# Latents, rotary keys and p: transposes by VectorE in 32x32 blocks instead of TensorE, in one inference step on one core

## The chip, the cores and the metric

The kernel runs on one core of a Trainium2 chip. The metric is the device time of one execution in microseconds (us); the median of several runs is given. The core has five engines that run side by side: TensorE (PE; its weight loads are shown apart as PEld), VectorE (DVE), ScalarE (ACT), GpSimd (POOL) and SyncE (SP), which here issues nearly all DMA transfers. Each engine works through its own queue in order, and waits at an instruction until what it needs is there.

## The reference, cut to what matters

One layer of a decoder for a prompt of 1024 tokens and 8 sampled sequences of 4 tokens each. The rows that the change touches:

```python
z = rmsnorm(x, ln_w) @ w_in
rq, rk, rv, rg, cq, ckv, kr, mg, ga, gb = jnp.split(z, ...)
q = (rmsnorm(cq, q_norm_w) @ w_uq).reshape(b, s, MLA_HEADS, MLA_QK)
ckv = rmsnorm(ckv, kv_norm_w)
kr = rope(kr, pos)                       # one rotary key of 64 for all heads
...
kv = (ckv @ w_ukv).reshape(b, s, MLA_HEADS, MLA_NOPE + MLA_V)
sc = einsum('bqhd,bkhd->bhqk', qn, k_nope) + einsum('bqhr,bkr->bhqk', qr, kr)   # masked softmax, then @ v
...
x = x + merged @ w_out
return x + jax.nn.sigmoid(x @ w_ple_gate) * (ple @ w_ple_proj)                 # ple is p, 256 wide
```

cq (384 wide), ckv (256) and kr (64) together are the 704 columns called latents here. The rest (retention with its state, paged attention of the samples, gates, the output projections) is computed too, and is not touched.

## The kernel before, in words

Arithmetic is done on pairs of fp32r tiles (a high part and the rest, `h` and `l`); a product is three matmuls (`mac`, lines 266 to 268). Matmuls need the contracted dimension on the 128 partitions. So what is computed with tokens on partitions has to be transposed before it can be multiplied further.

The stages, in order of time:

1. Latents, 0 to about 145 us. The prompt is worked through in 8 tiles of 128 tokens, and a ninth of 32 for the samples, in the order 0, 1, 8, 2 to 7. For a tile, `load_x` asks for x, `turn_tile` transposes it on TensorE (8 transposes, copied out of PSUM to `turn`, stored to `xTD`) and takes its norm, `scale_tile` makes `y` and the pair `xn`, and `latent_tile` multiplies by the latents' weights (48 matmuls into two PSUM tiles `ac`) and makes `la`: norms, rotation of the key (`rope_nat`, tiles `kro`), stores to the outputs. Then come, with a delay of one tile (the `yield` in `latent_tile` and `due` in `latents`), five transposes of `la` on TensorE, copies to `lt`, and a store to `latD`. The rotary key goes untransposed to `krD`. `turn_p` loads 128 rows of p to `pl`, has TensorE transpose them (two transposes), copies and stores them to `pTD`. The product `fill` (gates ga, gb, silu gates; tiles `mm`, results `gev`) is woven in from the seventh tile on.
2. First queries of the samples (weights `early`), paged attention with the rest of `fill` beside it, to about 750 us; retention, to about 1360 us.
3. Latent attention of the prompt, 8 heads, from about 1360 us. Latents are loaded transposed from `latD` (tiles `lat`, split to `lh` and `ll`). `rope_keys` transposes the key `krN` on TensorE and makes the pair `krA`, `krB`, each twice on 64 partitions. `prep` of a head is woven into the attention of the head before. For a block of 128 queries `probabilities` computes scores in `ac`, their maximum `mx` and minus that as `nm` (VectorE), the exponential `pr` (ScalarE) and the scaling by `rl` (GpSimd); `attend` transposes and multiplies by the values.
4. Output projections, to the end, where `embedding` loads p transposed from `pTD`.

The tile framework orders each engine's queue ahead of time, by a simulated schedule; so a change in one place moves instructions in its neighbourhood. Tiles of one tag form a ring of `bufs` buffers: a new one waits until the oldest is read. `wst` holds the rings of weights (`wr`, 2 buffers; `wh`, `wl`) and `gev` (2).

The pattern that the change uses is in the kernel already, for the retention's keys: VectorE's transpose turns each 32x32 block in place, and four stores, one for each group of 32 partitions, put the blocks where they belong in DRAM:

```python
dve.transpose(st, dst[m][:, j * TH:j * TH + n].rearrange("p (b r) -> p b r", r=32))
for a in range(0, P, 32):
    sp.dma_start(kD[h % 2][bs, :, m * P + a:m * P + a + 32].rearrange("b i f -> i b f"), st[a:a + 32])
```

Of the kernel before, what the change touches and what calls it, by code (L numbers as in the profile page):

```python
# [9 lines left out]
F32 = mybir.dt.float32  # L10
# [9 lines left out]
P = 128  # L20
# [141 lines left out]
def decode_step(ctx: ExitStack, tc: tile.TileContext, A: dict, O: dict):  # L162
# [57 lines left out]
    latD = dram.tile([P, 5, SEQ], F32, tag="latD", name="latD")  # L220
    xTD = dram.tile([P, 8, NT], F32, tag="xTD", name="xTD")
    pTD = dram.tile([P, 2, NT], F32, tag="pTD", name="pTD")
    krD = dram.tile([P, 8, ROPE], F32, tag="krD", name="krD")
# [104 lines left out]

    def turn_p(t):
        n = rows(t)  # L330
        pl = p1.tile([P, PLE], F32, tag="pl", name="pl", bufs=2)
        sp.dma_start(pl[:n], A["p_prompt"][0, 0, t * P:(t + 1) * P, :] if t < 8 else A["p_sample"].rearrange("l b t c -> (l b t) c"))
        turn_input(t, pl, pTD, PLE // P)
# [47 lines left out]
    def latent_tile(t):  # L381
# [15 lines left out]
        if t < 8:  # L397
            sp.dma_start(O["ckv_prompt"][0, 0, t * P:(t + 1) * P, :], kv)
            sp.dma_start(O["krope_prompt"][0, 0, t * P:(t + 1) * P, :], la[:, QL + KL:])
            sp.dma_start(krD[:, t, :], la[:, QL + KL:])  # L400
            yield
            pt, pt2 = tr(), tr()
            for i in range(3):
                pe.transpose(pt[:, i * P:(i + 1) * P], la[:, i * P:(i + 1) * P], ident)
            for i in range(2):
                pe.transpose(pt2[:, i * P:(i + 1) * P], la[:, (3 + i) * P:(4 + i) * P], ident)
            lt = p1.tile([P, 5, P], F32, tag="lt", name="lt", bufs=2)
            act.copy(lt[:, 0:3, :], pt[:, :3 * P].rearrange("p (a b) -> p a b", a=3))
            dve.tensor_copy(lt[:, 3:5, :], pt2[:, :2 * P].rearrange("p (a b) -> p a b", a=2))
            sp.dma_start(latD[:, :, t * P:(t + 1) * P], lt)  # L410
        else:
            sp.dma_start(O["ckv_sample"].rearrange("l b t c -> (l b t) c"), kv)
            sp.dma_start(O["krope_sample"].rearrange("l b t c -> (l b t) c"), la[:n, QL + KL:])
# [47 lines left out]
    def latents():  # L461
        due = iter(())
        for n, t in enumerate(order):
            tile_ = latent_tile(t)
            if 0 < n < 7:
                turn_tile(order[n + 2])
            next(tile_, None)
            run(due)
            due = tile_
# [4 lines left out]
            if n + 4 < 9:  # L474
                load_x(order[n + 4])
            turn_p(t)
# [6 lines left out]
        run(due)  # L483
# [598 lines left out]
    for h in range(HR):  # L1082
# [5 lines left out]
        if h + 1 < HR:  # L1088
            rest = (head_in(h + 1, nxt), 50.3)
        else:  # L1090
            rest = (gate_tiles(C_MG, mgD, range(5, 8), AF.Silu), 31.8)
            raws = [(qkB if i < 4 else qkA)("lat", (P, SEQ), F32) for i in range(5)]
            for i, raw in enumerate(raws):
                sp.dma_start(raw, latD[:, i, :])
            krN = qkA("krN", (P, 8, ROPE), F32)
            sp.dma_start(krN, krD)
# [43 lines left out]
    def rope_keys():  # L1140
        for u in range(2):
            pt = tr()
            us = slice(u * 512, (u + 1) * 512)
            for i in range(4):
                pe.transpose(pt[:ROPE, i * P:(i + 1) * P], krN[:, 4 * u + i, :], ident)
            act.copy(krA[0:ROPE, us], pt[:ROPE])
            act.copy(krA[ROPE:P, us], pt[:ROPE])
            lo_of(krB[0:ROPE, us], pt[:ROPE], krA[0:ROPE, us])
            act.copy(krB[ROPE:P, us], b32(krB[0:ROPE, us]))
            yield 0.43  # L1150
# [213 lines left out]
    waiting = []  # L1364
    for h in range(HM):
# [15 lines left out]
        for n, m in enumerate((3, 2, 0, 1)):  # L1381
# [9 lines left out]
            waiting.append(unit)  # L1391
            if h + 1 == HM:
# [92 lines left out]
    def embedding(j):  # L1485
        pT = [xs_("pT", (P, 2, TH)) for _ in range(2)]
        for k in range(2):
            hi, lo = (pT[k][:, i, :] for i in range(2))
            raw = xs_("pTr", (P, TH), F32)
            sp.dma_start(raw, pTD[:, k, j * TH:(j + 1) * TH])  # L1490
# [139 lines left out]
```

## Time and profile before

| | |
|---|---|
| median of 3 runs | 2164.25 us (2162.3 to 2164.99) |
| profiled execution | 2169.16 us |
| its span, first to last instruction | 2167.2 us |
| mean granted TensorE clock | 0.997 |
| TensorE busy | 2123.5 us, 15258 matmuls and transposes |
| VectorE busy | 1255.8 us |
| ScalarE busy | 730.7 us |
| DMA | 307.59 MB, mean 142 GB/s |

A row of the profile names line, engine and operation, output<-inputs by the program's names, shapes and count; then times. A busy TensorE is not one at its peak, as matmuls are pipelined: a matmul's printed length is longer than the distance to the next one's start, which is called its pitch below. Idle time in square brackets stands with the instruction that ended it and the operation that released it.

### The profile page before, as it was taken

What the parts mean: (1) busy time and instruction counts of PE and PEld (TensorE: products, weight loads), DVE (VectorE), ACT (ScalarE), POOL (GpSimd) and SP (SyncE); (2) the same over time, 40 slices, a digit from 0 to 9 for tenths busy, and PEclk for the clock granted to TensorE, in tenths of its full rate; (3) what the DMA queues carried; (4) which work ended last, traced back from release to release, by engine and by line L of the source; (5) the groups of instructions that cost most, each with busy time, mean ns of one, the idle gap of its engine ahead of it and who ended that gap; (6) DMA issues with size and microseconds to landing.
All of it is one profiled execution on the core that took longest, in us unless ns stands there. A gap on an engine that the chain in (4) does not pass through costs nothing.

```text
span 2167.2 us, 38594 instructions
## 1 busy us (share of the span) xinstructions
PE 2123.5 (98%) x15258; PEld 1847.5 (85%) x15258; DVE 1255.8 (58%) x2823; ACT 730.7 (34%) x1535; POOL 328.0 (15%) x519
## 2 busy tenths in 40 slices
PE   8999999999999999999999999899999999999998
PEld 7988777777777897888888887788888999999998
DVE  5524564565646346666676774778777353444465
ACT  6412222333334222222222221454556342222243
POOL 2210111111110022222122220122221000000022
PEclk9999999999999999999999999999999999999999
DMA  8557656566655432453634627110112453234243
GB/s 232 146 162 256 227 205 225 179 249 214 215 201 195 128 85 66 153 161 98 224 72 123 199 72 260 44 37 12 38 53 71 142 189 99 86 93 125 79 142 118
DMA packets 302693, 307.59 MB, mean 142 GB/s; under 512 B 61296, under 2 KB 260080, under 8 KB 298416
## 3 DMA queue, kind: packets, MB, share of 16 engines
q1 hardware_dynamic: 293296, 221.23, 33.6%
q0 software_dynamic: 9216, 83.89, 10.3%
q8 instruction: 120, 1.97, 0.4%
q14 instruction: 61, 0.50, 0.1%
HBM read 236.70 MB, written 68.36 MB: 141 GB/s over the span
## 4 chain that ended last, share of the span: by engine, by line
PE 63%; DVE 3%; issue 3%; ACT 1%; POOL 1%; DMA 1%; POOLq 0%; ACTq 0%; SPq 0%; DVEq 0%
PE mm L266 16%; PE mm L268 15%; PE mm L267 15%; PE ac L268 2%; PE ac L267 2%; PE ac L266 2%; PE mm L1329 2%; PE tr L1315 1%; PE sc L666 1%; PE ac L1272 1%; PE x L697 1%; PE tr L876 1%; PE ac L898 1%; PE ac L1273 1%; PE ac L1274 1%
## 5 line engine op out<-in xcount | busy, mean ns | idle before, releaser
L266 PE MATMUL mm<-xh,wh 128*128 128x352 f32 x1344 | 456.0, 339 | 1.6 <-ACT gev L421 0.7
L267 PE MATMUL mm<-xl,wh 128*128 128x352 f32 x1344 | 435.3, 324 | 0.0
L268 PE MATMUL mm<-xh,wl 128*128 128x352 f32 x1344 | 434.6, 324 | 0.0
L266 PEld LDWEIGHTS mm<-xh,wh 128*128 128x128 f32 x1344 | 252.4, 188 | 93.7 <-issue 79.0
L267 PEld LDWEIGHTS mm<-xl,wh 128*128 128x128 f32 x1344 | 253.6, 189 | 3.3 <-issue 1.0
L268 PEld LDWEIGHTS mm<-xh,wl 128*128 128x128 f32 x1344 | 253.2, 188 | 1.0 <-issue 0.6
L199 DVE TENSOR_TENSOR wl<-wr,wh 128x512 fp32r<-128x512 f32 (+2 forms) x251 | 174.2, 707 | 129.6 <-ACT wh L247 103.9
L247 ACT CAST wh<-wr 128x512 fp32r<-128x512 f32 x216 | 129.8, 618 | 296.9 <-PE mm L267 217.7
L662 DVE STREAM_TRANSPOSE kt<-craw 128x512 f32<-128x512 f32 x256 | 160.7, 680 | 107.3 <-PE sc L666 74.6
L421 ACT ACTIVATE gev<-mm 128x352 f32<-128x352 f32 x120 | 55.6, 464 | 227.0 <-PE mm L268 149.0
L268 PE MATMUL mm<-mh,wl 128*128 128x352 f32 x384 | 124.3, 324 | 0.0
L268 PE MATMUL mm<-gh,wl 128*128 128x352 f32 x384 | 124.3, 324 | 0.0
L266 PE MATMUL mm<-mh,wh 128*128 128x352 f32 x384 | 124.3, 324 | 0.0
L266 PE MATMUL mm<-gh,wh 128*128 128x352 f32 x384 | 124.2, 324 | 0.0
L267 PE MATMUL mm<-ml,wh 128*128 128x352 f32 x384 | 124.2, 324 | 0.0
L267 PE MATMUL mm<-gl,wh 128*128 128x352 f32 x384 | 124.2, 323 | 0.0
L266 PE MATMUL mm<-wv,xh 128*128 128x512 f32 x256 | 103.8, 405 | 0.0
L267 PE MATMUL mm<-wv,xh 128*128 128x512 f32 x256 | 100.9, 394 | 0.0
L268 PE MATMUL mm<-wv,xl 128*128 128x512 f32 x256 | 100.7, 393 | 0.0
L666 PE MATMUL sc<-kt,q 32*32 32x512 f32 x2560 | 95.6, 604 | 1.0 <-DVE kt L662 1.0
L865 ACT ACTIVATE on<-ac,gb,gs 128x512 f32<-128x512 f32 (+1 forms) x36 | 28.0, 778 | 179.9 <-DVE gb L863 179.7
L1560 POOL TENSOR_TENSOR xr<-x1h,x1l 128x352 f32<-128x352 f32 x24 | 27.1, 1153 | 389.3 <-DVE pT L199 311.2
(392 smaller groups left out, 4559.6 us busy)
## 6 DMA issues: line engine op xcount, KB each, us to landing
wr<-in_w_in_dram SPq DMA_DIRECT2D x144, 256.0 KB
st<-in_state_ret_dram SPq DMA_DIRECT2D x32, 512.0 KB
out_ret_sample_dram<-st SPq DMA_DIRECT2D x32, 512.0 KB
wr<-in_w_ple_gate_dram SPq DMA_DIRECT2D x48, 256.0 KB
gt<-gev SPq DMA_DIRECT2D x48, 176.0 KB
gl<-go SPq DMA_DIRECT2D x16, 528.0 KB
gate<-ga SPq DMA_DIRECT2D x16, 528.0 KB
g<-gt SPq DMA_DIRECT2D x32, 256.0 KB
```

What stands on the lines that cost most here:

```text
L199: dve.tensor_tensor(out=out, in0=src, in1=b32(hi), op=ALU.subtract)
L247: hi_by[0](hi, raw)
L266: pe.matmul(out, wh, xh, start=first, stop=False)
L267: pe.matmul(out, wh, xl, start=False, stop=False)
L268: pe.matmul(out, wl, xh, start=False, stop=last)
L421: act.activation(t, ps, func)
L662: dve.transpose(kt[:, 2 * i + s].rearrange("p (n r) -> p n r", r=32), src)
L666: pe.matmul(sc[32 * v:32 * v + 32, q, :], Q["q4"][qs_, j + v // 2, 2 * (g % 2) + v % 2, :], kt[qs_, v, :], start=n == 0, stop=n == NJ // 2 ...
L697: pe.matmul(pv[32 * v:32 * v + 32, :KL], pT[:, n, 32 * v:32 * v + 32], keys[v % 2][:, 8 * (v // 2) + n, :], start=n == 0, stop=n == 7, til ...
L865: act.activation(on[:n], po, AF.Identity, bias=nb[:n], scale=s[:n])
L1329: pe.matmul(po[:, :256], v[a][w], t[:, x, 256 * a:256 * a + 256], start=j + a + part == 0, stop=False, skip_group_check=True)
L1560: pool.tensor_tensor(out=xr, in0=b32(x1[f][0][:, sl]), in1=b32(x1[f][1][:, sl]), op=ALU.add)
```

## The change

Four things. `latent_tile` has VectorE transpose all 704 columns of `la` in 32x32 blocks, and four stores place them in `latD`, which now holds the key too; the five TensorE transposes, two copies, the store to `krD` and the delay of one tile are gone. `rope_keys` takes the key transposed from `latD`, loaded twice (`krT`), and needs only a split. `turn_p` does the same for p with tiles `pl` and `tp` in the ring `gev`, and is called in the attention, in heads 1 to 5, instead of in the latents. `load_x` is called at the head of a tile's turn.

```diff
-    latD = dram.tile([P, 5, SEQ], F32, tag="latD", name="latD")
+    latD = dram.tile([NLAT // 32, 32, SEQ], F32, tag="latD", name="latD")
-    pTD = dram.tile([P, 2, NT], F32, tag="pTD", name="pTD")
-    krD = dram.tile([P, 8, ROPE], F32, tag="krD", name="krD")
+    pTD = dram.tile([PLE // 32, 32, NT], F32, tag="pTD", name="pTD")
...
+    def turn_blocks(dst, st, src, t, n):
+        st = st.rearrange("p (b r) -> p b r", r=32)
+        dve.transpose(st[:n], src[:n].rearrange("p (b r) -> p b r", r=32))
+        for a in range(0, n, 32):
+            sp.dma_start(dst[:, :, t * P + a:t * P + a + 32].rearrange("b i t -> i b t"), st[a:a + 32])
+
     def turn_p(t):
         n = rows(t)
-        pl = p1.tile([P, PLE], F32, tag="pl", name="pl", bufs=2)
+        pl, tp = (wst.tile([P, PLE], F32, tag="gev", name=name, bufs=2) for name in ("pl", "tp"))
         sp.dma_start(pl[:n], ...)
-        turn_input(t, pl, pTD, PLE // P)
+        turn_blocks(pTD, tp, pl, t, n)
...
             sp.dma_start(O["krope_prompt"][0, 0, t * P:(t + 1) * P, :], la[:, QL + KL:])
-            sp.dma_start(krD[:, t, :], la[:, QL + KL:])
-            yield
-            pt, pt2 = tr(), tr()
-            for i in range(3):
-                pe.transpose(pt[:, i * P:(i + 1) * P], la[:, i * P:(i + 1) * P], ident)
-            for i in range(2):
-                pe.transpose(pt2[:, i * P:(i + 1) * P], la[:, (3 + i) * P:(4 + i) * P], ident)
-            lt = p1.tile([P, 5, P], F32, tag="lt", name="lt", bufs=2)
-            act.copy(lt[:, 0:3, :], pt[:, :3 * P].rearrange("p (a b) -> p a b", a=3))
-            dve.tensor_copy(lt[:, 3:5, :], pt2[:, :2 * P].rearrange("p (a b) -> p a b", a=2))
-            sp.dma_start(latD[:, :, t * P:(t + 1) * P], lt)
+            turn_blocks(latD, p1.tile([P, NLAT], F32, tag="lt", name="lt", bufs=2), la, t, P)
...
     def latents():
-        due = iter(())
         for n, t in enumerate(order):
-            tile_ = latent_tile(t)
+            if n + 4 < 9:
+                load_x(order[n + 4])
             if 0 < n < 7:
                 turn_tile(order[n + 2])
-            next(tile_, None)
-            run(due)
-            due = tile_
+            latent_tile(t)
             if n == 0:
                 turn_tile(order[2])
             if n < 7:
                 scale_tile(order[n + 2])
-            if n + 4 < 9:
-                load_x(order[n + 4])
-            turn_p(t)
...
-                sp.dma_start(raw, latD[:, i, :])
-            krN = qkA("krN", (P, 8, ROPE), F32)
-            sp.dma_start(krN, krD)
+                sp.dma_start(raw, latD[4 * i:4 * i + 4].rearrange("b i t -> (b i) t"))
+            krT = qkA("krT", (P, SEQ), F32)
+            for r in range(0, P, ROPE):
+                sp.dma_start(krT[r:r + ROPE], latD[20:].rearrange("b i t -> (b i) t"))
...
     def rope_keys():
         for u in range(2):
-            pt = tr()
             us = slice(u * 512, (u + 1) * 512)
-            for i in range(4):
-                pe.transpose(pt[:ROPE, i * P:(i + 1) * P], krN[:, 4 * u + i, :], ident)
-            act.copy(krA[0:ROPE, us], pt[:ROPE])
-            act.copy(krA[ROPE:P, us], pt[:ROPE])
-            lo_of(krB[0:ROPE, us], pt[:ROPE], krA[0:ROPE, us])
-            act.copy(krB[ROPE:P, us], b32(krB[0:ROPE, us]))
-            yield 0.43
+            split(krT[:, us], krA[:, us], krB[:, us])
+            yield 0.1
...
-    waiting = []
+    waiting, turning = [], list(range(9))
     for h in range(HM):
...
         for n, m in enumerate((3, 2, 0, 1)):
...
             waiting.append(unit)
+            if 0 < h < HM - 1 and n in (1, 3) and turning:
+                turn_p(turning.pop(0))
...
-            sp.dma_start(raw, pTD[:, k, j * TH:(j + 1) * TH])
+            sp.dma_start(raw, pTD[4 * k:4 * k + 4, :, j * TH:(j + 1) * TH].rearrange("b i t -> (b i) t"))
```

How the order of instructions moves, at three places. First TensorE in the latents, while tile 8 (32 rows, `ac` of 32x384) follows tile 1. Before (`pl`, `xt`, `la` are transposes of p, x and the latents, `rs_r` the norm's factor spread by a matmul):

```order
L267 MATMUL ac<-wll_203,xh_117 32x384
L323 MATMUL tr<-cst,pl 128x128 x2
L323 MATMUL tr<-cst,xt 128x128 x8
L404 MATMUL tr<-cst,la 128x128 x3
L406 MATMUL tr<-cst,la 128x128 x2
L268 MATMUL ac<-wlh_202,xl_118 32x384
L350 MATMUL tr<-cst,rs_r_426 128x128
L266 MATMUL ac<-wlh_208,xh_119 32x384
L323 MATMUL tr<-cst,pl 128x128 x2
L323 MATMUL tr<-cst,xt 128x128 x4
```

After, at the end of tile 1 and the start of tile 8:

```order
L267 MATMUL ac<-wlh_233,xl_127 128x320
L355 MATMUL tr<-cst,rs_r_424 128x128
L322 MATMUL tr<-cst,xt 128x128 x8
L265 MATMUL ac<-wlh_187,xh_112 32x384
L266 MATMUL ac<-wll_188,xh_112 32x384
```

The transposes of `pl` and `la` are gone, and those of x stand further ahead. The last tile's transposes of `la` stood behind 81 matmuls `mm` of the gates. On SP the same stage has four stores to `latD` per tile where one stood, and the loads of the gates' weights `wr` later: before, the first four stand ahead of the third prompt tile's `latD` store; now the first two stand behind the fourth tile's, and the next two behind the sixth's and two stores of `ga`.

Second, VectorE at the attention's first blocks. Before (`mx` is the maximum, `nm` minus that, `rl` the reciprocal sum; `k` the low part of the next head's keys):

```order
L1279 TENSOR_REDUCE mx<-ac 128x1 x2
L1280 ISA ac,mx<-ac,above,mx 128x448
L1280 ISA mx 128x1
L199 TENSOR_TENSOR k<-mm,k 128x512
L1283 TENSOR_SCALAR nm<-mx 128x1
L1292 TENSOR_TENSOR l<-l 128x1
L1294 RECIPROCAL rl<-l 128x1
L1280 ISA ac,mx<-ac,above,mx 128x512
L1280 ISA mx 128x1
L1283 TENSOR_SCALAR nm<-mx 128x1
```

After:

```order
L199 TENSOR_TENSOR k<-mm,k 128x512
L199 TENSOR_TENSOR qr<-tr,qr 64x512
L1263 TENSOR_REDUCE mx<-ac 128x1 x2
L1264 ISA ac,mx<-ac,above,mx 128x448
L1264 ISA mx 128x1
L330 STREAM_TRANSPOSE tp<-pl 128x256
L1267 TENSOR_SCALAR nm<-mx 128x1
L1276 TENSOR_TENSOR l<-l 128x1
L1278 RECIPROCAL rl<-l 128x1
L1264 ISA ac,mx<-ac,above,mx 128x512
L1264 ISA mx 128x1
L330 STREAM_TRANSPOSE tp<-pl 128x256
```

Transposes of p (the fourth and fifth of nine) stand between the maximum and `nm`, and `k` has moved ahead of the maxima. Third, SP there, after (before, the weight loads `wr` follow each other without the rows of p):

```order
L337 DMA pl<-in_p_prompt_dram 128x256
L245 DMA wr<-in_w_ukv_dram 128x2x128
L332 DMA pTD<-tp 32x8x32 x2
L245 DMA wr<-in_w_ukv_dram 128x2x128
L332 DMA pTD<-tp 32x8x32 x2
L337 DMA pl<-in_p_prompt_dram 128x256
L332 DMA pTD<-tp 32x8x32 x4
L337 DMA pl<-in_p_prompt_dram 128x256
L332 DMA pTD<-tp 32x8x32 x4
```

The third load of p, its four stores with a weight load between them, the fourth load, and so on: each load stands behind the stores of the one before, and those wait for VectorE.

More of the change, by code (lines that the diff above doesn't have):

```diff
@@ L482, in latents @@
             yield 7.1 if n > 5 else 0.0
-        run(due)
     beside(latents(), 3 * 7.1, fill, 36)
```

## The prediction

> **What bounds the kernel.** First the page's busy times (engine, busy us, share of the span, instructions) and its chain that ended last.
>
> ```profile
> span 2167.2 us, 38594 instructions
> PE 2123.5 (98%) x15258; PEld 1847.5 (85%) x15258; DVE 1255.8 (58%) x2823; ACT 730.7 (34%) x1535; POOL 328.0 (15%) x519
> PE 63%; DVE 3%; issue 3%; ACT 1%; POOL 1%; DMA 1%; POOLq 0%; ACTq 0%; SPq 0%; DVEq 0%
> ```
>
> TensorE is busy for 98% of the span and carries the chain, so an instruction taken from it is worth its pitch wherever TensorE waits for nobody. Then I read windows over the changed stages: the latents (27 to 145 us) and the start of the latent attention (from 1360).
>
> ```profile
> 27.00:60.00 33.00, 31.06 (x205) 27.36 (x206) 18.61 (x70) 21.95 (x66) 7.91 (x22) 1.00 0.82 227
> 60.00:145.00 85.00, 84.80 (x544) 83.28 (x543) 31.77 (x94) 26.60 (x76) 15.08 (x32) 1.00 0.41 120
> 1360.00:1391.00 31.00, 28.44 (x185) 24.60 (x183) 29.52 (x80) 14.92 (x27) 5.43 (x10) 1.00 0.22 64
> ```
>
> After window and length stand the busy times of PE, PEld, DVE, ACT and POOL, the clock, the DMA share, GB/s. The latents are bound by TensorE (84.80 of 85.00 us, VectorE 31.77). The attention's start is bound by VectorE: 29.52 of 31.00 us, with gaps on TensorE. The change relieves TensorE in the first place and loads VectorE in the second.
>
> **Transposes of latents and p: the gain.** Gone from TensorE between 34 and 143 us are 40 transposes of `la` and 18 of `pl` (two of them 32 rows). One group of seven in its timeline (start, length, line, operation):
>
> ```profile
> 128.78 0.31 PE L268 MATMUL ac<-wlh,xl 128*128 128x320 f32 x1
> 128.92 0.49 PE L404 MATMUL tr<-cst,la 128*128 128x128 f32 x3
> 129.25 0.38 PE L406 MATMUL tr<-cst,la 128*128 128x128 f32 x2
> 129.47 0.38 PE L323 MATMUL tr<-cst,pl 128*128 128x128 f32 x2
> 129.61 0.41 PE L266 MATMUL mm<-xh,wh 128*128 128x352 f32 x1
> 129.85 0.32 PE L267 MATMUL mm<-xl,wh 128*128 128x352 f32 x1
> ```
>
> A matmul of 320 columns has a pitch of 0.15 us, one of 352 of 0.16 (starts of neighbours), so without the seven the `mm` of 129.85 would have started at 128.78 + 0.15 + 0.16 = 129.09. Seven cost 0.76 us, 0.109 each; 56 full ones make 6.1 us, the two small ones an estimated 0.1: **-6.2 us**. The ends are 0, if something else comes to bound the stage, and -9.5 us, if the printed length (0.49 for three) were the cost; the pitch is what TensorE's next instruction sees, so I take it.
>
> **One wait there.** Between 28 and 143 us TensorE's timeline has one idle stretch over 0.2 us:
>
> ```profile
> 48.76 0.28 PE L323 MATMUL tr<-cst,pl 32*128 32x32 f32 x2 [1.20 <-ACT xh L358]
> ```
>
> The instruction that waits, a transpose of `pl`, goes away; the x transposes behind it move ahead with their loads, and ScalarE, named as the releaser, loses its copies of `lt` and of p's `turn`. Ends 0 and -1.2; I take **-1.2**, since the next instruction there is a matmul whose x tile is ready sooner than before.
>
> **What VectorE pays there.** Eight transposes of 704 columns replace eight copies of 425 ns:
>
> ```profile
> L821 DVE STREAM_TRANSPOSE kb<-k x24: 469/508/547, 799.6 to 1247.0; 128x352 f32<-128x352 f32 x16, 128x320 f32<-128x320 f32 x8
> L662 DVE STREAM_TRANSPOSE kt<-craw 128x512 f32<-128x512 f32 x256 | 160.7, 680 | 107.3 <-PE sc L666 74.6
> L409 DVE COPY lt<-tr x8: 418/425/425, 36.4 to 143.5; 128x256 f32<-128x256 f32 x8
> ```
>
> 508 ns at 352 columns and 680 at 512 give 1.07 ns a column: an estimated 0.89 us at 704 and 0.41 at 256. That is 0.46 us more a tile, priced at **0** because VectorE is busy for 18.61 of 33 us; uncovered it would delay the next tile's `y` and `xl` by 0.46 each, 3.7 us over eight.
>
> **Stores of 128-byte pieces.** The kernel has such stores, kD<-kb; first their issue by SP (min/median/max ns), then a window of them:
>
> ```profile
> L823 SPq DMA_DIRECT2D kD<-kb x96: 302/462/1641, 800.2 to 1251.6; - x96
> 801.00:803.00 2.00, 2.00 (x14) 2.00 (x13) 0.38 (x1) 0.00 (x0) 0.00 (x0) 1.00 0.54 90
> ```
>
> 90 GB/s take 0.54 of the engines, so 167 GB/s would fill them. A tile's four `latD` stores carry 352 KB (704 pieces of 128 bytes each): 2.2 us of all engines. What leaves the stage per tile (p's load and store, 128 KB each, `krD` 32 KB, the old `latD` 320 KB) is 608 KB at 227 GB/s / 0.82 = 277 GB/s: also 2.2 us. So the DMA share stays at 0.82, and the cost is **0**. The Trainium skill speaks against the change here ("DMA: Bandwidth & Descriptors", Specifications: below 512 bytes a transfer leaves the line rate and becomes a read-modify-write). The row agrees in kind, 167 against 277 GB/s, but not in a way that changes the sum; what a stronger penalty would do is a rival below. SP issues about 2 us of stores per tile and loses four issues of about 0.5: even.
>
> **The first queries.** The `early` weights may land only when this stage's pool is free. SP, then TensorE:
>
> ```profile
> 144.05 0.52 SPq L410 DMA_DIRECT2D latD<-lt  x1
> 147.52 2.29 SPq L526 DMA_DIRECT2D early<-in_w_uq_dram  x4
> 152.07 0.81 PE L538 MATMUL mm<-early 128*32 128x384 f32 x2 [1.11 <-ACT gev L421]
> 157.01 0.83 PE L538 MATMUL mm<-early 128*32 128x384 f32 x2 [0.40 <-DMA early<-in_w_uq_dram]
> ```
>
> The last `latD` store waited for transposes that stood behind 81 matmuls; now it follows its tile. The load comes earlier against TensorE; the two waits of 1.5 us may go or stay. I take half: **-0.8**.
>
> **Rotary keys.** TensorE and GpSimd at the attention's start:
>
> ```profile
> 1359.73 1.03 PE L1145 MATMUL tr<-cst,krN 128*64 128x128 f32 x8
> 1361.05 0.35 PE L266 MATMUL ac<-wqr,lh 128*128 128x256 f32 x1 [0.28 <-POOL wqr L196]
> 1359.98 1.31 POOL L196 TENSOR_SCALAR wqr<-wr 128x256 fp32r<-128x256 f32 x3
> ```
>
> The eight `krN` transposes (0.9 us by the pitch) fill a time in which TensorE would wait for `wqr` anyway: it waits 1.2 us instead of 0.28. Worth **0**; ends 0 and -0.9. Six casts of ScalarE become two, off the path. `krB` stays two subtractions of 512 columns; one moves ahead of `wqr`, where VectorE is idle.
>
> **p in the attention: the cost.** Nine transposes (8 x 0.41) stand in VectorE's queue from about 1376 on. The first three cost 1.2 us less the 0.6 of the moved `krB`, and are covered by an idle 1.17 us ahead of `qr`. The fourth and fifth stand between a maximum and its `nm`, for which ScalarE's exponential waits, and for that TensorE. VectorE, TensorE, SP, and a load's landing:
>
> ```profile
> 1392.67 0.68 DVE L199 TENSOR_TENSOR qr<-tr,qr 64x512 fp32r<-64x512 f32 x1 [1.17 <-ACT qr L1240]
> 1397.04 0.14 DVE L1280 DVE_READ_ACCUMULATOR2_ANT mx<- 128x1 f32 x1
> 1397.04 0.69 DVE L199 TENSOR_TENSOR k<-mm,k 128x512 fp32r<-128x512 f32 x1
> 1397.64 0.14 DVE L1283 TENSOR_SCALAR nm<-mx 128x1 f32<-128x1 f32 x1
> 1401.55 0.14 DVE L1280 DVE_READ_ACCUMULATOR2_ANT mx<- 128x1 f32 x1
> 1398.60 0.53 PE L1272 MATMUL ac<-k,q 128*128 128x512 f32 x1 [2.96 <-ACT pr L1290]
> 1405.11 0.88 PE L1315 MATMUL tr<-cst,pr 128*128 128x128 f32 x6 [0.49 <-POOL pr L1295]
> 1393.97 0.37 SPq L246 DMA_DIRECT2D wr<-in_w_ukv_dram  x1
> 1361.60 0.38 SPq L246 DMA_DIRECT2D wr<-in_w_uq_dram  x1
> 1364.29 1.62 POOL L196 TENSOR_SCALAR wh<-wr 128x384 fp32r<-128x384 f32 x2 [2.24 <-DMA wr<-in_w_uq_dram]
> ```
>
> A load issued at 1361.60 is used at 1364.29: 2.7 us. On SP the fourth `pl` load stands behind the weight load of 1393.97 and two stores (0.46 each): issued at 1395.3, landed at 1398.0. VectorE is ready for it at 1397.2: 0.8 us of waiting and 0.41 of work, less 0.60 as `k` no longer stands in that gap: `nm` 0.6 later. The fifth load stands behind four stores: 1398.4 + 1.9 + 2.7 = 1403.0; VectorE would be ready at 1401.7 + 0.6 = 1402.3: wait 0.7, work 0.41: 1.1 later. The sixth's load lands at 1403.4 + 4.6 = 1408.0, before its place: 0.4. The last three lie where TensorE does not wait. TensorE waits for this chain at 1398.60 and 1405.11, so I take it in full: **+2.1**. Ends 0 (TensorE has other work queued) and 9 x (0.41 + 2.7) = +28, every load waited for in full. `wr` loads behind p's stores are used a head later.
>
> **Sum.** -6.2 - 1.2 - 0.8 + 0 + 2.1 = -6.1 us. The profiled execution took 2169.16 us (2.0 beside its span), the median of the runs is 2164.25: 2163.1 for such an execution, **2158.1 us** as median. A measurement here tells about 0.2% (4.3 us) from no change.
>
> **Rivals.**
> - The attention hides p: SP and VectorE run ahead, and TensorE's gaps take it. -8.2: 2156.0 us. For it speaks TensorE's other work of the next head; against it the 2.96 us gap.
> - The latents give half back (0.17). SP now loads the gates' second weight pair behind two `ga` stores, where four loads stood ahead of the first gate. One such load, exposed, is 2.7 + 0.8 (a cast) = 3.5 us; the last third of the gate's tile covers most of it. Uncovered: -6.1 + 3.5 = -2.6, 2161.6 us, no difference.
> - The early stores fill the DMA engines (0.08). If 128-byte pieces cost twice the row's 2.2 us, four tiles bring 8.8 us more into a window of 33 with 6 free: +2.8, 2160.9 us, no difference. The row of kD<-kb, 0.54 at 90 GB/s, speaks against it. This is what the Trainium skill's rule named above would do here (same page and section).
> - Slower: `pl` loads land late. The fourth to sixth transposes hold `nm` back by whatever a load takes beyond 2.7 us, so y us more cost 3y: the sum is zero at y = 2.0, and at y = 4 (6.7 us to land) it is +5.9: 2170.2 us. Against it: the DMA share of 0.22 there.
> - That the change does not do what it says is excluded: TensorE's order has 66 transposes less.
>
> **Numbers.** Forecast 0.45, p hidden 0.19, late weights 0.17, full DMA engines 0.08, slower 0.11. Faster: 0.45 + 0.19 = 0.64; same 0.17 + 0.08 = 0.25; slower 0.11. The range leaves out the slower case and the tails of the others: from 2154.0 (p hidden, the first queries' 1.5 us in full and the 0.9 of `krN` make 2154.4) to 2164.5, which holds the cases without difference and 2.9 us more, one further exposed load.
>
> **What would show it.** Right: no `la` or `pl` transposes on TensorE, the first `mm<-early` about 8 us sooner, the attention's first `nm` under 1 us later against its stage's start, TensorE's gap before 1398.60 grown to 3 to 4 us. Wrong: idle TensorE for `wh` or `wl` between 75 and 140 us; VectorE waiting for `pl` by more than 2 us; a DMA share near 1 before 60 us.

## The result, and the profile after

The changed kernel takes 2153.16 us, the median of five runs (2150.59 to 2154.09), against 2164.88 of the kernel before beside it: ratio 0.9949, interval 0.9937 to 0.9961, 11.7 us less. The forecast was 2158.1, and the time lies 0.8 us below the low end of its range. The profiled execution took 2150.59 us. First the lines of its page that answer to those shown of before (span, busy times, chain):

```profile
span 2148.7 us, 38490 instructions
PE 2107.3 (98%) x15192; PEld 1841.5 (86%) x15192; DVE 1261.0 (59%) x2832; ACT 723.7 (34%) x1514; POOL 326.4 (15%) x519
PE 87%; DVE 2%; ACT 1%; DMA 1%; issue 1%; POOL 1%; SPq 0%; ACTq 0%; DVEq 0%; POOLq 0%
```

TensorE has 66 instructions less and is still the bound. The windows over the changed stages (window and length, then busy PE, PEld, DVE, ACT, POOL, clock, DMA share, GB/s):

```profile
27.00:60.00 33.00, 32.54 (x203) 29.95 (x204) 20.58 (x74) 19.64 (x59) 7.01 (x19) 0.95 0.73 160
60.00:145.00 85.00, 79.64 (x502) 78.36 (x500) 34.35 (x95) 23.38 (x66) 18.34 (x42) 1.00 0.51 135
1340.00:1371.00 31.00, 28.77 (x176) 25.71 (x177) 29.36 (x78) 11.65 (x22) 5.55 (x9) 0.94 0.31 83
```

The DMA engines are less busy in the first window than before (0.73 for 0.82), though their pieces are smaller: 160 GB/s at 0.73 would be 219 when full, for 277 before. In the second window TensorE now has gaps (79.64 of 85.00). Its timeline names them:

```profile
27.46 0.40 PE L355 MATMUL tr<-cst,rs_r 32*128 32x32 f32 x2 [1.91 <-POOL rs_r L234]
78.31 0.49 PE L355 MATMUL tr<-cst,rs_r 128*128 128x128 f32 x2 [3.28 <-POOL rs_r L234]
90.38 0.43 PE L267 MATMUL mm<-xh,wl 128*128 128x352 f32 x1 [1.46 <-DVE wl L199]
108.49 0.43 PE L267 MATMUL mm<-xh,wl 128*128 128x352 f32 x1 [0.62 <-DVE wl L199]
```

The wait for the norm `rs_r` at 78 us and the two for `wl` are new: 5.4 us. For the first `wl` the weights had long landed (their load is issued at 70.19 us). VectorE has no idle stretch from 78.80 to 92 us, and `wl` stands in its queue behind two of the new transposes, of which the second is:

```profile
88.26 0.90 DVE L330 STREAM_TRANSPOSE lt<-la 128x704 f32<-128x704 f32 x1
89.66 0.67 DVE L199 TENSOR_TENSOR wl<-wr,wh 128x512 fp32r<-128x512 f32 x1
```

VectorE's new instructions (min/median/max ns) and, from SP and TensorE, the early loads and their first user:

```profile
L330 DVE STREAM_TRANSPOSE tp<-pl x9: 423/436/448, 1355.5 to 1409.5; 128x256 f32<-128x256 f32 x8, 32x256 f32<-32x256 f32 x1
L330 DVE STREAM_TRANSPOSE lt<-la x8: 895/900/911, 29.0 to 131.2; 128x704 f32<-128x704 f32 x8
138.44 0.38 SPq L515 DMA_DIRECT2D early<-in_w_uq_dram  x1
141.34 1.71 SPq L515 DMA_DIRECT2D early<-in_w_uq_dram  x3
148.75 0.84 PE L527 MATMUL mm<-early 128*32 128x384 f32 x4
```

The estimates of 0.89 and 0.41 us were 0.900 and 0.436. The early loads come 6 to 9 us sooner than before (147.52), and their users wait for nothing. Of the forecast's signs, TensorE's gap at the attention's start came (3.1 us); the first `mm<-early` is 3.3 us sooner than before (148.75 for 152.07), not 8; and a sign of being wrong came too, TensorE idle for `wl` at 90 and 108 us.

To see where the time went, one profile against one is not enough. The table has the lengths of five stretches (us), cut at instructions: on TensorE the start of the transposes of `latS` (the samples' latents), the first score matmul `sc` of the page attention, its last value matmul, the first product with `wqr`; at the end ScalarE's last write of the output `o`. "Fills" is the kernel before with a small addition (experiment 6); the other columns are the two kernels, each time as profiled.

| stretch | before, three profiles (the third with fills) | after, four profiles | means differ by | forecast |
|---|---|---|---|---|
| start to latS | 143.4, 147.5, 144.8 | 141.3, 140.3, 140.9, 140.5 | -4.5 | -7.4 |
| latS to `sc` | 57.1, 58.5, 57.0 | 53.0, 53.1, 53.1, 53.0 | -4.5 | -0.8 |
| page attention | 537.3, 534.7, 526.6 | 524.9, 534.1, 524.8, 526.5 | about -1.5, see below | 0 |
| to `wqr` (retention) | 623.2, 629.3, 625.9 | 621.9, 623.1, 622.8, 623.4 | -3.3 | 0 |
| `wqr` to the end | 800.8, 800.8, 799.7 | 802.2, 803.5, 803.3, 802.1 | +2.3 | +2.1 |

The sum of the means, -11.5, agrees with the medians. The 18.5 us between the two first profiles do not: their page attentions differ by 12.4 us with the same code and order. In some sessions, that is runs made one after another on one chip (before: 2171.9 and 2171.4 us), VectorE goes on late behind each chunk's last score matmul, in others (2163.8, 2164.7, 2164.0) it doesn't, and the profiled execution of before (2169.16) is of the first kind. Such places are called late ends below. So the page attention is compared within a kind: 536.0 to 534.1 with late ends, 526.6 (the kernel with fills) to 525.4 without. All ratios below are against runs of before in the same session.

### The profile page after: what moved, and what is told of

It reads as the page before. It is cut to its first block, busy times and chain, and to the rows that moved or that the text cites. A ratio compares the mean times of both kernels' runs of the same rounds, so it can differ in the third digit from the quotient of the medians.

```text
span 2148.7 us, 38490 instructions
## 1 busy us (share of the span) xinstructions
PE 2107.3 (98%) x15192; PEld 1841.5 (86%) x15192; DVE 1261.0 (59%) x2832; ACT 723.7 (34%) x1514; POOL 326.4 (15%) x519
## 4 chain that ended last, share of the span: by engine, by line
PE 87%; DVE 2%; ACT 1%; DMA 1%; issue 1%; POOL 1%; SPq 0%; ACTq 0%; DVEq 0%; POOLq 0%
PE mm L265 22%; PE mm L266 20%; PE mm L267 20%; PE sc L655 4%; PE x L686 3%; PE ac L267 2%; PE ac L265 2%; PE ac L266 2%; PE mm L1313 2%; PE tr L1299 1%; PE tr L865 1%; PE ac L1038 1%; PE ac L1256 1%; PE x L680 1%; PE ac L887 1%
## 5 line engine op out<-in xcount | busy, mean ns | idle before, releaser
L655 PE MATMUL sc<-kt,q 32*32 32x512 f32 x2560 | 91.2, 600 | 0.0
```

The lines of the kernel that those rows point to most:

```text
L655: pe.matmul(sc[32 * v:32 * v + 32, q, :], Q["q4"][qs_, j + v // 2, 2 * (g % 2) + v % 2, :], kt[qs_, v, :], start=n == 0, stop=n == NJ // 2 ...
```

## The experiments

**1 and 2. The two kernels again.** Was the page attention the gain? Here is one late end in the profile before (from the timelines of TensorE, GpSimd and VectorE):

```profile
308.45 1.14 PE L666 MATMUL sc<-kt,q 32*32 32x512 f32 x32
308.76 0.94 POOL L602 DMA_INDIRECT rraw<-in_cache_krope_dram,idx  x1 [14.20 <-DVE kt L662]
310.00 0.94 POOL L602 DMA_INDIRECT rraw<-in_cache_krope_dram,idx  x1 [0.30 <-issue]
311.56 1.31 DVE L662 STREAM_TRANSPOSE kt<-craw 128x512 f32<-128x512 f32 x2 [2.47 <-remote]
```

and the same place after:

```profile
302.23 1.14 PE L655 MATMUL sc<-kt,q 32*32 32x512 f32 x32
303.56 1.30 DVE L651 STREAM_TRANSPOSE kt<-craw 128x512 f32<-128x512 f32 x2 [0.69 <-PE sc L655]
```

After, VectorE goes on 0.2 us behind the matmuls (302.23 + 1.14 = 303.37, 303.56). Before, it goes on 2.0 us behind them (309.59, 311.56), 0.6 after the second gather.

> The kernel before, once more, for a second profile. The gain that the forecast has no term for lies in the page attention, whose code is untouched: from its first score matmul to its last value matmul 537.3 us in the profile before, 524.9 after. In the profile before, 14 of its score matmuls (one of each chunk of pages) tell VectorE of their end 1 to 2.4 us late; after, none does. Theory A (it belongs to the kernel before): again about 14 late ones, the stage 535 to 539 us. Rival B (it belongs to that one execution, the slowest of five): fewer than 5 late ones, the stage 525 to 530 us, the whole under 2164 us.

> The changed kernel once more, for a second profile. Theory A: no late ones, page attention 524 to 526 us, the whole 2150 to 2154. Rival B: some late ones are as likely here as before, the stage 525 to 535 us.

Measured: both profiles have late ends, the page attention took 534.7 and 534.1 us, the executions 2178.05 and 2161.33 (median of before there: 2171.92). Neither theory of mine held: the late ends go with the chip or the session, not with the kernel, and after, in this one execution, keeps its distance with them (10.6 us to that median). They are not the gain.

**3 and 4. Parts undone.** `p_back` undoes p alone (TensorE turns it in the latents, called at the end of a tile's turn), `latents_back` undoes latents and keys:

```diff
 p_back, against the changed kernel
-        turn_blocks(pTD, tp, pl, t, n)
+        turn_input(t, pl, pTD, PLE // P)
...
             if n < 7:
                 scale_tile(order[n + 2])
+            turn_p(t)
```

> The changed kernel with p alone undone: p is transposed by TensorE in the latents as before, nothing of it is in the attention. By the forecast's terms TensorE pays 16 x 0.109 + 0.1 = 1.9 us in the latents and the attention gives back 2.1: 0.2 us below the changed kernel, 2153; by the attention's stretch as profiled (from the stage's start to the first product of queries 1.5 us longer) 0.4 above it, 2153.5. If the page attention's gain of 6 us (between medians) hangs on p's leaving the latents: 2159.

> The changed kernel with the latents and the keys undone: TensorE transposes them as before, with the delay of a tile; p stays in the attention, x is asked for at the head. By the forecast's terms TensorE is relieved of p's 1.9 us and perhaps of the wait of 1.2 us, and pays 1.5 to 2.1 in the attention: 1.0 to 1.6 us below the kernel before, 2163.5. If the page attention's gain of 6 us hangs on p: 2157.5.

Measured: `p_back` 2181.87, ratio to before 1.0047 (1.0035 to 1.0059), some 21 us above the changed kernel where I expected none or 6. `latents_back` 2173.9, 1.0006 (0.9997 to 1.0015): p's move and x at the head alone bring nothing. In `p_back` the first score matmul comes at 212.6 us instead of 194. SP and TensorE there (`xt` are x's transposes):

```profile
70.03 2.52 SPq L332 DMA_DIRECT2D latD<-lt  x4
72.64 0.51 SPq L337 DMA_DIRECT2D pl<-in_p_prompt_dram  x1
40.95 0.38 PE L322 MATMUL tr<-cst,pl 128*128 128x128 f32 x2
41.17 1.04 PE L322 MATMUL tr<-cst,xt 128*128 128x128 f32 x8
45.40 0.69 PE L265 MATMUL ac<-wlh,xh 128*128 128x384 f32 x1 [2.56 <-ACT xh L363]
61.09 0.44 PE L265 MATMUL ac<-wlh,xh 128*128 128x384 f32 x1 [3.54 <-ACT xh L363]
```

p's loads stand on SP behind the four stores of `lt`, which wait for `la`. But TensorE waits for a landing of p only once, 0.9 us; the load issued at 32.62 us is used at 40.95. What differs is the order of TensorE's queue: a tile's x transposes stand behind p's, and both behind all matmuls of the tile ahead. The third prompt tile's come at 41.17 us instead of 29.96, the fourth's at 56.17 instead of 35.52. So the way from x's transposes to `xh` lies open, and TensorE waits for it. Up to latS its waits (from 20 us on) sum to 15.9 us instead of 7.3, and half clock (stretches with a granted clock of 0.5) costs 8.5 us instead of 1.7 (the sum of 1 minus the granted clock over windows of 1 us). That the framework put the queue in this order because p's loads come late on SP fits, but is not shown: no run has p in the latents with its loads ahead of the stores.

**5, 6 and 7. The late ends taken away?** In `rr_before` and `rr_after` GpSimd fills a buffer ahead of the gathers of 12 of the 16 chunks; every other engine's order stays.

```diff
-        cr = [big("craw", (NA * KL,)) for _ in range(2)]
+        cr, _ = [big("craw", (NA * KL,)) for _ in range(2)], [pool.memset(rr[0], 0.0) if jj else None]
```

> The changed kernel against the one before, timed in five rounds, with a third profile of it. In the profile of its first execution no score matmul of the page attention told VectorE late of its end (stage 524.9 us), in the second 21 did (534.1). The late ones all end 0.57 us after the second of GpSimd's two gathers of rotary rows (rraw). Theory A (the gain between medians is the page attention's state, which changes from execution to execution): with late ones the ratio is near 0.9985 (2.5 to 3 us), without them 0.994. Theory B (the gain lies in the start of the kernel): the ratio is 0.994 to 0.996 whatever the state.

> The kernel before, where in 12 of the 16 chunks of pages GpSimd fills the buffer of rotary rows with zeros ahead of its gathers, which delays these by some 1.1 us, past the end of the last score matmul; the order of every other engine is as it was. If the gathers hold the matmul's semaphore: at most 6 late ones are left, the page attention takes 526 to 529 us instead of 534 to 537, the ratio to before is 0.996 to 0.997. If they don't, the stage stays at 534 or above and the ratio at 1.000.

> The changed kernel with the same 12 fills ahead of the gathers. If the gathers hold the semaphore: at most 6 late ones, page attention 526 to 529 us, and 6 to 7 us below the changed kernel when that runs with late ones, else the same as it.

Measured: after 2152.32, ratio 0.9950 (0.9937 to 0.9963); `rr_before` 0.9998 (0.9989 to 1.0007); `rr_after` 0.9948 (0.9935 to 0.9961). No profile of these three runs has late ends, also not at the four chunks without a fill; the chip bears the same number as that of experiments 1 and 2. So the fills had nothing to remove, and what makes the ends late stays open. For the change it settles this: Theory A is out. Without late ends the ratio is 0.9950, and the one execution with them (`after_again`) stands at 0.9951 of its median of before.

**8 and 9. x at the end, and x at the head alone.** `x_tail` is the changed kernel with `load_x` at the end of a tile's turn, `x_head_only` the kernel before with it at the head:

```diff
 x_head_only, against the kernel before
+            if n + 4 < 9:
+                load_x(order[n + 4])
             tile_ = latent_tile(t)
```

> The changed kernel with x asked for at the end of a tile's turn, as before. My forecast had no term for this part; if it matters, x lands later behind the stores of 128-byte pieces and TensorE waits for x's transposes between 27 and 60 us: 1 to 3 us above the changed kernel. If not: the same as it within 1 us.

> The kernel before with one edit: x asked for at the head of a tile's turn instead of its end. Undoing the same edit in the changed kernel cost 8 us. Theory A (x at the head helps only because VectorE's latents put four stores, which wait for la, ahead of x on SP): here, with one latD store for a tile, the ratio is 0.998 to 1.002. Theory B (x is late in both kernels and the edit is a gain by itself): 0.996 to 0.997, 6 to 8 us.

Measured: `x_tail` 2160.77, 0.9981 (0.9973 to 0.9990), 8.4 us above the changed kernel; `x_head_only` 2166.91, 1.0011 (1.0001 to 1.0020). This fits Theory A. SP and TensorE of `x_tail`:

```profile
63.88 2.36 SPq L332 DMA_DIRECT2D latD<-lt  x4
66.34 0.51 SPq L302 DMA_DIRECT2D xt<-in_x_prompt_dram  x1
75.12 0.50 SPq L302 DMA_DIRECT2D xt<-in_x_prompt_dram  x1
55.85 1.03 PE L322 MATMUL tr<-cst,xt 128*128 128x128 f32 x8
59.22 0.49 PE L355 MATMUL tr<-cst,rs_r 128*128 128x128 f32 x2 [2.33 <-POOL rs_r L234]
84.57 0.80 PE L355 MATMUL tr<-cst,rs_r 128*128 128x128 f32 x2 [3.73 <-POOL rs_r L234]
```

and SP and TensorE of the changed kernel:

```profile
49.38 0.38 SPq L302 DMA_DIRECT2D xt<-in_x_prompt_dram  x1
57.58 2.10 SPq L332 DMA_DIRECT2D latD<-lt  x4
59.77 0.50 SPq L302 DMA_DIRECT2D xt<-in_x_prompt_dram  x1
45.01 1.03 PE L322 MATMUL tr<-cst,xt 128*128 128x128 f32 x8
```

The last two x tiles are asked for 17.0 and 15.3 us later in `x_tail`, behind the stores. From 27 us on no row of TensorE waits for x to land here either; its queue has another order. The fifth prompt tile's transposes stand at 55.85 us instead of 45.01, the seventh's at 79.81 instead of 64.15, and behind each of them TensorE waits for the norm of x. latS comes 8.0 us later than in after's mean: TensorE's waits before it (from 20 us on) sum to 9.3 us instead of 7.3, and half clock costs 8.5 us instead of 1.7. With the runs so far, the parts (L latents and keys, P p, X x at the head) as ratios to before: X 1.0011, P+X 1.0006, L+X 1.0047, L+P 0.9981, all three 0.9949. Without L the other two are worth nothing; with it P is worth 21 us and X 8. L alone was not run.

**10, 11 and 12. What is left in the changed kernel.** `x5` asks for x one tile earlier still, `p_late` puts p's work into the output projections, in a ring that is free only after the attention, `x5_p_late` does both.

```diff
 x5
-            if n + 4 < 9:
-                load_x(order[n + 4])
+            if n + 5 < 9:
+                load_x(order[n + 5])
 p_late
-        pl, tp = (wst.tile([P, PLE], F32, tag="gev", name=name, bufs=2) for name in ("pl", "tp"))
+        both = w4("pl", (P, 2, PLE), F32)
+        pl, tp = both[:, 0], both[:, 1]
```

> The changed kernel with x asked for one tile earlier still (the ring of four holds it). TensorE's wait of 3.28 us for x's norm (rs_r) at 78 us should go, and the half clock behind the idle time with it: 3 to 5 us below the changed kernel, ratio to before 0.9925 to 0.9935. If the DMA engines, 0.7 busy there, are what makes x late, no gain: 0.995.

> The changed kernel with p's nine transposes and stores moved out of the attention's start, into the output projections (their buffers are taken from a ring that is free only after the attention). If they cost the attention what the forecast says, 2.1 us, this gives 2.1 less than the changed kernel, ratio 0.994; if the attention hides them, the same as the changed kernel.

> Both edits on the changed kernel: x one tile earlier, p in the output projections. If both of their costs stand, 5 to 7 us below the changed kernel, ratio to before 0.992.

Measured: 2154.11, 2154.22, 2154.69; all three 0.9951 (intervals within 0.9937 to 0.9965): no gain. `x5` asks for its last x tile at 48.1 us instead of 59.8, and TensorE's wait stays. Its SP group (first and last start) and its waits (us, times, longest):

```profile
L302 SPq DMA_DIRECT2D xt<-in_x_prompt_dram x5: 425/480/2558, 19.5 to 48.1; - x5
PE tr L355 <- POOL rs_r L234: 5.1, 2, 3.2
```

So x's landing isn't what the norm waits for. ScalarE of the changed kernel shows what is:

```profile
75.19 0.49 ACT L398 ACTIVATE la<-ac 128x384 f32<-128x384 f32 x1 [3.81 <-DMA wr<-in_w_in_dram]
75.67 1.05 ACT L347 ACTIVATE xs<-xt 128x1024 f32<-128x1024 f32 x1
76.83 1.06 ACT L347 ACTIVATE xs<-xt 128x1024 f32<-128x1024 f32 x1
```

The Squares of x stand behind a square of `la` that waits 3.81 us. (The releaser is printed as a DMA; what `la` needs is the product `ac`.) For p: the last stretch takes 801.1 us in `p_late` and 801.0 in `x5_p_late`, against 802.8 of after, which the timing here can't tell from 0. That stretch goes with the half clock in it, over all 20 profiles (its cost counted as above, over the first 795 us):

| cost of half clock, us | profiles | last stretch, us |
|---|---|---|
| 0 | `rr_before` | 799.7 |
| 1.7 | before, `before_again`, `x_head_only`, `p_late`, `x5_p_late` | 800.8 to 801.1 |
| 3.4 | `p_back` and nine with p in the attention | 801.2, 801.5 to 802.2 |
| 5.1 | `x_tail`, `late_lat` | 802.5, 803.6 |
| 6.8 | `after_timed`, `after_again` | 803.3, 803.5 |

The half clock stands in the first 8 us of the stretch, behind a wait for `wqr`, and some 36 to 47 us into it, behind the wait for `pr`. All 13 profiles with p in the attention have 3.4 us or more, six of the seven others 1.7 or none. At the same half clock `p_back`, with p in the latents, is 0.7 us below the mean of the nine. So what p's place costs, 1 to 2 us, comes mostly with half clock; whether p brings that on, no row shows. TensorE's waits in the attention's first 59 us, of before, after and `p_late`:

```profile
PE ac L1272 <- ACT pr L1290: 3.0, 1, 3.0
```

```profile
PE ac L1256 <- ACT pr L1274: 4.1, 2, 3.1
```

```profile
PE ac L1257 <- ACT pr L1275: 3.8, 2, 3.4
```

The largest wait is there without p too (3.4 in `p_late`, 3.1 in after), so the 1 us that I had reckoned for p isn't there.

**13 and 14. The two mis-sized terms.** `dummy` puts 56 idle transposes back on TensorE, `late_lat` turns the last tile's latents the old way:

```diff
 dummy (in latent_tile, after rope_nat)
+        if t < 8:
+            for w in (4, 3):
+                pt = tr()
+                for i in range(w):
+                    pe.transpose(pt[:, i * P:(i + 1) * P], ident, ident)
```

> The changed kernel with seven idle transposes (of the identity, read by nobody) put on TensorE for each of the eight prompt tiles in the latents: the 56 that the change took away, without their copies and loads. By the forecast's pitch, 56 x 0.109 = 6.1 us above the changed kernel (2158.5 beside 2152.3). If TensorE's waits for x's norm and for the gates' weights hide them (5.4 us between 27 and 110 us), 1 to 3 us. If the 4 us that the untouched stages gained hang on the time at which they start, these stages grow too: above 8 us.

> The changed kernel with the last prompt tile's latents turned the old way: six transposes on TensorE behind the gates' matmuls, copies, and six stores ahead of the early weights' loads. My forecast gave the earlier loads 0.8 us; by the profiles the stretch from latS's transposes to the first score matmul is 57.0 to 58.5 us before and 53.0 to 53.1 after. If the loads' start is the cause: this stretch is 56 to 58 us and the whole 3 to 5 us above the changed kernel. If not: 1 us (the six transposes).

Measured: `dummy` 2175.37, 1.0023 (1.0013 to 1.0033), some 15 us above the changed kernel (0.9949 x 2171.42 = 2160.3). Its latS comes at 147.5, 6.8 us later than after's mean: 0.12 a transpose, so the pitch of 0.109 was about right, by one profile. But latS to `sc` takes 57.2 instead of 53.0, page attention 1.5 and retention 2.9 more than after. `late_lat` 2167.45, 0.9981 (0.9972 to 0.9991), 7 us above: latS at 141.4, but 56.7 us from there to `sc`, as before the change. SP and TensorE of `late_lat`, then the wait in `dummy`:

```profile
141.64 2.85 SPq L484 DMA_DIRECT2D latD<-lt  x6
146.22 2.00 SPq L527 DMA_DIRECT2D early<-in_w_uq_dram  x4
150.69 0.80 PE L539 MATMUL mm<-early 128*32 128x384 f32 x2 [1.81 <-DMA early<-in_w_uq_dram]
159.15 2.12 PE L539 MATMUL mm<-early 128*32 128x384 f32 x18 [0.49 <-DMA early<-in_w_uq_dram]
```

```profile
159.66 0.83 PE L532 MATMUL mm<-early 128*32 128x384 f32 x2 [2.44 <-DMA early<-in_w_uq_dram]
```

So the later start of the early loads costs 3.6 us in that stretch, not 0.8. In all 13 other profiles with VectorE's latents the stretch takes 53.0 or 53.1 us, whether latS comes at 137.6 or at 159.6; in the five with TensorE's latents it takes 57.0 to 59.4. In `dummy` the last three early loads start as in the changed kernel, 0.1 us behind latS, and one of them is waited for all the same, with half clock behind it that costs 1.7 us: the changed kernel has little to spare here.

**15 to 18. The order on ScalarE.** `sq_all` orders the Square of x ahead of the squares of `la` of its turn; `x5_sq` adds `x5`.

```diff
-        act.activation(xs[:n], xt[:n], AF.Square, accum_out=ss[:n])
+        squares.append(act.activation(xs[:n], xt[:n], AF.Square, accum_out=ss[:n]).ins)
...
-            act.activation(dst, src, AF.Square, accum_out=ss[:n])
+            with tc.issue_after(squares[-1]) if len(squares) > 2 else ExitStack():
+                act.activation(dst, src, AF.Square, accum_out=ss[:n])
```

> The changed kernel with ScalarE's Square of x (for its norm) ordered ahead of the squares of la of the tile before, in every tile. In its profiles the last two Squares stand behind a square of la that waits 3.7 us for the latents' product, and TensorE then waits 3.28 us for the norm; asking for x earlier did not help. If the order on ScalarE is the cause: that wait goes, and the half clock after it, latS starts 3 to 5 us sooner, ratio to before 0.993. If x lands late: no gain.

> Both: x asked for one tile earlier, and the Squares ahead. 3 to 5 us below the changed kernel, or 1 more than with the order of the Squares alone, where x's landing is next in line.

> The changed kernel once more, beside the kernel with both edits (x one tile earlier, Squares ahead), on one chip. Ratio to before 0.994 to 0.996. Late ones in its profile if the chip shows them in the other kernel's profile too, none if not: by the runs so far the state goes with the chip and the call, not with the kernel.

> The changed kernel with x asked for one tile earlier and the Squares ahead of la's. By the profiles so far the first score matmul comes 1 to 3 us sooner than in the changed kernel (192.6 and 191.2 for the order alone, against 193.4 to 194.3): 1 to 3 us below the changed kernel in the same call.

Measured: `sq_all` 2158.73, 0.9946 (0.9930 to 0.9962); `x5_sq` 2158.66, 0.9944 (0.9928 to 0.9959), both on a chip where before takes 2171.42. On another one, together: after 2152.69, 0.9949 (0.9935 to 0.9962), and `x5_sq` 2150.23, 0.9938 (0.9924 to 0.9952). The wait at 78 us is gone; ScalarE and TensorE of `sq_all`, then TensorE's waits of `x5_sq` in the last run between 20 and 200 us:

```profile
72.17 1.06 ACT L347 ACTIVATE xs<-xt 128x1024 f32<-128x1024 f32 x1 [4.53 <-DVE own L432]
74.33 0.49 PE L355 MATMUL tr<-cst,rs_r 128*128 128x128 f32 x2 [0.22 <-POOL rs_r L234]
```

```profile
PE tr L355 <- POOL rs_r L234: 2.4, 2, 1.9
PE mm L267 <- DVE wl L199: 2.3, 2, 1.6
```

The first score matmul comes at 190.6 us instead of 193.5, and the median of the whole is 2.5 us lower, as expected of the last run; the 3 to 5 us expected of the first two did not come. The runs and intervals of after and `x5_sq` overlap, so a gain of the whole is not shown; that the wait at 78 us hung on ScalarE's order is. Next in line at that place is the buffer of `xs`: `own`, of the page table, lies in the same ring. Another buffer for it wasn't tried. The last two runs also fit the finding on late ends: none in either profile, and 2164.0 for before.

## Why the prediction was short

The forecast's sum was -6.1 us; -11.7 was measured. The errors partly cancel: the start up to latS gained 2.9 us less than forecast, the first queries 3.7 more, and 4.8 came in stages that had no term. By its steps:

- **58 transposes, -6.2.** The price was about right: `dummy` pays 0.12 for each of 56. The stage did not keep all of it: start to latS gained 4.5 us, not 7.4 with the next term.
- **The wait at 48.76, -1.2.** It went. That another one would not come was wrong: 3.28 for the norm, 1.46 and 0.62 for `wl`. The wait for the norm had no rival: ScalarE's Square of x stands behind a square of `la` (`sq_all` removes the wait). The longer one for `wl` looks like the rival of late gate weights and isn't, as those weights had landed; VectorE's queue was late.
- **VectorE's transposes and the 128-byte stores, 0 each.** For the DMA engines this held: the share went down to 0.73, and the rival of full engines fell. For VectorE it did not quite: two transposes stand ahead of the `wl` for which TensorE waits 1.46 us; how much of that is theirs, no run separates. And it was left out that SP issues the stores in order, and that they wait for `la`. x's move ahead of them, which I had costed at nothing, is worth 8 us (`x_tail`), and p's move out of the latents 21 (`p_back`), both through another order of TensorE's queue and the half clock behind its waits.
- **The first queries, -0.8.** This is the step that failed most: latS to `sc` gained 4.5 us (4.0 without the half clock in one of the profiles of before), with every profile of after within 0.1 of the others. I halved two waits of 1.5 us, and so bounded the term by the two rows I had quoted, of which the longer, 1.11, is printed with `gev` as its releaser and not a load. All waits of that stretch in before sum to 2.6 us, and after has none. The rest shows only as longer busy time of TensorE (54.40 us against 52.86, with nearly the same instructions). `late_lat` gives 3.6 us back by delaying these loads.
- **Rotary keys, 0.** The wait is as forecast: TensorE waits 1.70 for `wqr` instead of 0.28 with the 0.9 of `krN` gone; I had 1.2. The half clock behind it was left out: in 10 of the 15 profiles with keys from `latD`, all four of after among them, it follows within 8 us and costs 1.7 or 3.4 us, and in none of the five with `krN`. No run changes the keys alone.
- **p in the attention, +2.1.** The last stretch grew by 2.3, and that the size came out is luck. The chain given for it (the maximum's `nm` held back by 1 us) is not in the rows, and timed, p's removal showed no gain. The growth goes with half clock, by the table above, which the forecast had nowhere: behind the wait for `wqr` and behind that for `pr`.
- **Stages that the change does not touch, no term.** The page attention gained about 1.5 us, 1.7 us of half clock in the first profile of before included, and the retention 3.3. With the changed kernel's code in the retention, the eleven profiles whose first score matmul came by 194.4 us took 621.9 to 624.9 there, and the four where it came at 198.1 or later (`late_lat`, `x_tail`, `dummy`, `p_back`) 625.7 to 627.2. The code of before took 623.2 to 629.3 without such an order (623.2 at 200.5 us). So a late start goes with a longer retention in the changed kernel; by what, I did not settle. TensorE's waits there sum to 3.7 to 4.8 us in the eleven and 4.7 to 6.1 in the four, and half clock costs up to 1.7 and 3.4.
- **The base.** The terms were read from one execution of before that started early (200.5 us to `sc`, 201.8 and 206.0 in the two others) and had the late ends of the page attention. The forecast was set on the median of 2164.25, so the late ends did not move it, but the start that it priced was the shortest of three.

The range's low end, 2154.0, took in the first queries' 1.5 us, `krN` and hidden p, and nothing for a stage outside the change: with 3 us more for `early` it would have held the time.

## What to carry to other kernels

A store that waits for a late result delays the loads issued behind it on the same queue (x's last two by 15 and 17 us in `x_tail`), and the order in which a framework schedules the other engines moves with them. When work moves to another engine, list the loads that its stores now stand ahead of, move these first, and then compare the order of TensorE's queue; for x that was worth 8.4 us. Where a stretch shows several short waits that end in the same group of loads, price them together, and give the whole stretch as the bound. Take stage lengths from more than one profile before a sum is made against them, and count the half clock in each: here it orders the lengths of the last stretch, and a term came out right by it though its mechanism was wrong.

## What the runs showed of the hardware

- In some sessions on a chip, VectorE goes on behind a chunk's last score matmul only about 2 us after the printed end, 0.6 us after GpSimd's second gather (311.56 against 310.00 + 0.94), while the matmuls behind it start on time (309.52 in before). The row names no releaser on this core (it prints `remote`). The page attention takes 532 to 537 us in the nine profiles with late ends and 525 to 529 in the eleven without. The Trainium skill says that TensorE's end in a trace is a model and not a measurement ("Perfetto Trace Analysis", Tensor Engine Instruction), so the rows can't tell whether the matmul ended late or only its signal came late. No run here shows what makes it so.
- An idle stretch under 4 us can lose the clock for a while. `x_tail`, with its waits of 2.33 and 3.73 us, has in the windows behind them (columns as above) a granted clock of 0.84 and 0.83:

```profile
60.00:80.00 20.00, 19.61 (x108) 19.55 (x109) 11.58 (x39) 8.55 (x26) 2.52 (x7) 0.84 0.66 160
80.00:100.00 20.00, 16.25 (x89) 15.75 (x88) 14.98 (x45) 10.74 (x30) 6.41 (x16) 0.83 0.55 132
```

In windows of 1 us the clock there is 0.50 from 60 to 66 and from 84 to 90 us. In these traces such a stretch costs 1.7 us or 3.4, so it lasts about 3.4 or 6.8 us. It doesn't follow every wait: the first profile of the changed kernel has it behind the wait of 1.91 us at 27 us and not behind that of 3.28 at 78. What decides, no run here settles.
